# A 31-tap depthwise convolution on VectorE, accumulated in two PSUM banks instead of in SBUF

## The chip, the cores and the metric

The kernel runs on one core of a Trainium2 chip. The metric is the device time of one execution in microseconds (us), as the median of three executions. TensorE (PE in the profile) multiplies matrices, VectorE (DVE), ScalarE (ACT) and GpSimd (POOL) work on elements, SyncE (SP) only issues transfers. SBUF holds 128 partitions; PSUM has eight banks of 128 x 512 fp32.

## What is computed

One layer of a diffusion backbone. The latent stream has 1024 tokens of width 1024, on a grid of 16 rows of 64; there are 256 context tokens. The first half of the layer is

```python
def seq_conv(x, w, b, grid):
    bsz, length, ch = x.shape
    if grid:
        rows = length // GRID_W
        return dwconv(x.reshape(bsz * rows, GRID_W, ch), w, b).reshape(bsz, length, ch)
# mixing: h = modulate(rms_norm(x, g), shift, scale); one projection h @ w gives
#   a, gl         -> u = a * sigmoid(gl) -> seq_conv, width 31 along a grid row -> LayerNorm -> swish
#   q, k, v, gates -> 4 chunkwise mLSTM heads, both directions, started from the context's states
#   o             -> sigmoid gate of the heads' output
# both groups joined -> output projection; then an up/down feed-forward stage
# shift, scale and gates of each stage: six vectors of 1024, a product of silu(c) with w_ada
```

The convolution has 512 channels: four blocks of 128 partitions with 1024 tokens each. An output column of a row is a sum over up to 31 neighbours in that row.

## The kernel before, in words

**Products.** All data are fp32, and a product is made of three: a matrix is split into a high and a low part (`split`, L131 to L135: ScalarE rounds a raw block, and GpSimd or VectorE takes the difference, L134). The weights of a projection come in blocks of 128 x 1024 (`load_blk`) into a ring of three raw tiles, `rawp`.

**Stages, in order of time.** Up to 75 us: the input, its norm, its transposes, the modulation. 75 to 128: the projections a and gl in four blocks j; `glu_evac` (L271 to L274) writes u[j]. 127 to 215: `vpass` (L540 to L567, the projections of v and of the gates with tokens on the partitions), `ctx_prepare` (L335 to L363: the context rows are transposed on TensorE, L353, taken out of PSUM by L358, and split, L362 and L363) and `gates` (L572 to L657), a chain of short steps that goes to and fro between VectorE and TensorE. 215 to 310: the projections k and q (`proj`, L684), woven with `ctx_states` (L711, L713) and head 0 of `heads` (L784 to L823). Then `conv_norm` (L867 to L892) transposes the convolved channels, normalizes them and transposes them back. 325 to 463: heads 1 to 3, the projections of q and o and a part of the output projection; the first instruction that only this stage has is the head norm, L832. From 463 on: the output projection, the up and the down stage; TensorE is busy there nearly without a break.

**The convolution.** `conv(j)` (L276 to L287) begins with the middle tap on ScalarE, into an SBUF tile `accf[:, j]`, and adds the other 30 taps in place on VectorE, each one an instruction over 128 x 784 to 128 x 1008 elements (L286):

```python
act.activation(out=accf[:, j], in_=u[j], func=AF.Identity, scale=conv_w[:, j, 15:16], ...
dve.scalar_tensor_tensor(out=dst, in0=uv[...], scalar=conv_w[:, j, t:t + 1], in1=dst, ...
```

So a tap reads two SBUF tiles (u and the accumulator) beside the column of weights. All four are issued under the lowest priority.

**The later modulation sums.** `ada_stream` (L242 to L252) loads 32 rows of `w_ada` through the raw ring and sums each with one instruction on VectorE (`mod_sum`, L228: a product of 128 x 1024 with a running sum). `proj` takes two of them at each of its twelve calls (`ada_step(2)`), and `ada_step(100)` behind the heads takes what is left.

**What sets the order.** A scheduler fixes the order of the instructions of each engine when the kernel is built; it fills VectorE's gaps with the low-priority taps. The order of SP's transfers is that of the code. At run time an engine takes its instructions in the fixed order, and one that must wait holds up all behind it. A tile is taken from a pool; where all buffers of a pool are in use, the next user waits. PSUM is two pools of four banks each: `mm` for projections, `tp` for transposes, scores and states.

Of the kernel before, what the change touches and what calls it, by code (L numbers as in the profile page):

```python
# [13 lines left out]
P = 128  # L14
# [16 lines left out]
def hybrid_block(ctx: ExitStack, tc: tile.TileContext, x, cx, cc, small, gb, w_ada,  # L31
# [12 lines left out]
    mm = wide.enter_context(tc.tile_pool(name="mm", bufs=4, space=bass.MemoryType.PSUM))  # L44
    tp = wide.enter_context(tc.tile_pool(name="tp", bufs=4, space=bass.MemoryType.PSUM))
    early = ExitStack()
# [35 lines left out]
    def MM():  # L82
        return mm.tile([P, 512], F32, tag="mm", name="mm")

    def TP():
        return tp.tile([P, 512], F32, tag="tp", name="tp")

    def H2(n=512):
# [187 lines left out]
    def conv(j):  # L276
        uv = u[j].rearrange("p (r c) -> p r c", c=W)
        act.activation(out=accf[:, j], in_=u[j], func=AF.Identity, scale=conv_w[:, j, 15:16],
                       bias=conv_b[:, j:j + 1])
        for t in range(CW):  # L280
            o = t - 15
            if o == 0:
                continue
            lo, hi = max(0, -o), min(W, W - o)
            dst = accf[:, j].rearrange("p (r c) -> p r c", c=W)[:, :, lo:hi]
            dve.scalar_tensor_tensor(out=dst, in0=uv[:, :, lo + o:hi + o], scalar=conv_w[:, j, t:t + 1],  # L286
                                     in1=dst, op0=ALU.mult, op1=ALU.add)  # L287

# [42 lines left out]
    def ada_step(n):  # L331
        for _ in range(n):
            next(ada_g, None)
# [142 lines left out]
    for j in range(2):  # L476
        u[j] = T4()
        for hf in range(2):
            glu_evac(j, hf, *ps0[j, hf])
    accf = wide_tile(4, 2)  # L480
    vw = None
    with prio(100000):
# [196 lines left out]
    def proj(i, evac):  # L679
        w = ahead.pop(i)  # L680
        n = order.index(i) + 1
        if n < len(order):
            ahead[order[n]] = load_blk(order[n])
        ada_step(2)  # L684
        for hf in range(2):
            hi, lo = hT[hf]
            ps = MM()
            yield from mm_block(ps, w, hi, lo)
            evac(hf, ps)
        return w  # L690
# [53 lines left out]
    def mlstm_head(h):  # L744
# [38 lines left out]
        for g in range(2):  # L783
# [9 lines left out]
            for t in range(4):  # L793
# [3 lines left out]
                cs = slice(c * P, (c + 1) * P)  # L797
                pv, pc = TP(), TP()
                nv = pv[:, 0:258].rearrange("p (d n) -> p d n", d=2)
# [66 lines left out]

    def conv_norm():  # L867
        for hf in range(2):
            xh = [T4().rearrange("p (t n) -> p t n", n=512) for _ in range(2)]
# [662 lines left out]
```

## Time and profile before

| | |
|---|---|
| median of three executions | 1196.62 us (1196.0 to 1198.24) |
| the profiled execution | 1197.89 us, its span 1195.8 |
| TensorE busy | 1143.2 us, 96% of the span |
| VectorE busy | 932.0 us, 78% |
| ScalarE busy | 523.7 us, 44% |
| GpSimd busy | 121.3 us, 10% |

The span is the profiler's time from the first to the last instruction; 2.1 us of the execution lie around it, and the profiled execution is 1.27 us above the median. Busy shares are means over the whole span: VectorE's 78% is 98 to 100% in some stages and 60% in others.

### The profile page before, as it was taken

What the parts mean: (1) busy time and instruction counts of PE and PEld (TensorE: products, weight loads), DVE (VectorE), ACT (ScalarE), POOL (GpSimd) and SP (SyncE); (2) the same over time, 40 slices, a digit from 0 to 9 for tenths busy, and PEclk for the clock granted to TensorE, in tenths of its full rate; (3) what the DMA queues carried; (4) which work ended last, traced back from release to release, by engine and by line L of the source; (5) the groups of instructions that cost most, each with busy time, mean ns of one, the idle gap of its engine ahead of it and who ended that gap; (6) DMA issues with size and microseconds to landing.
All of it is one profiled execution on the core that took longest, in us unless ns stands there. A gap on an engine that the chain in (4) does not pass through costs nothing.

```text
span 1195.8 us, 14940 instructions
## 1 busy us (share of the span) xinstructions
PE 1143.2 (96%) x5463; PEld 939.5 (79%) x5463; DVE 932.0 (78%) x1702; ACT 523.7 (44%) x952; POOL 121.3 (10%) x106
## 2 busy tenths in 40 slices
PE   6899898999898999999999999999999999999997
PEld 5788787877687777887787888878888878888885
DVE  4899999999779996568966676676668685995585
ACT  6432222242485454357545344343434355454461
POOL 2634120111302210010000000000000000000000
PEclk9899899999999999999999999999999999999999
DMA  8963110442225412442324231323132159633251
GB/s 305 329 207 121 52 37 1 142 147 65 88 89 176 140 56 89 150 167 89 104 73 132 88 122 55 132 89 132 45 132 93 75 192 391 227 112 117 80 220 71
DMA packets 51823, 153.42 MB, mean 128 GB/s; under 512 B 5589, under 2 KB 5925, under 8 KB 49958
## 3 DMA queue, kind: packets, MB, share of 16 engines
q1 hardware_dynamic: 40662, 132.28, 32.0%
q10 hardware_dynamic: 11088, 20.19, 4.5%
q8 instruction: 43, 0.70, 0.2%
q14 instruction: 30, 0.25, 0.1%
HBM read 123.83 MB, written 28.61 MB: 127 GB/s over the span
## 4 chain that ended last, share of the span: by engine, by line
PE 61%; DVE 6%; ACT 1%; issue 1%; POOL 0%; DVEq 0%; POOLq 0%; ACTq 0%
PE mm L1141 8%; PE mm L1143 8%; PE mm L1142 8%; PE c L1369 3%; PE c L1371 3%; PE c L1370 3%; PE tp L1143 3%; PE tp L1142 3%; PE tp L1141 3%; PE a L1369 3%; PE a L1371 3%; PE a L1370 2%; PE mm L951 2%; PE mm L953 2%; PE mm L952 2%; PE tp L508 2%
## 5 line engine op out<-in xcount | busy, mean ns | idle before, releaser
L286 DVE SCALAR_TENSOR_TENSOR s<-t,sml,s 128x864 f32<-128x864 f32 (+14 forms) x120 | 150.5, 1295 | 0.1
L150 PE MATMUL mm<-s,w 128*128 128x512 f32 (+1 forms) x320 | 126.6, 399 | 0.0
L151 PE MATMUL mm<-s,w 128*128 128x512 f32 (+1 forms) x320 | 124.7, 393 | 0.1
L133 ACT ACTIVATE w<-raw 128x1024 fp32r<-128x1024 f32 x94 | 97.0, 1054 | 20.6 <-DMA raw<-in_w_out_dram 5.3
L1141 PE MATMUL mm<-s,w 128*128 128x512 f32 x264 | 104.9, 397 | 0.7 <-ACT h L1214 0.7
L1142 PE MATMUL mm<-s,w 128*128 128x512 f32 x264 | 104.2, 395 | 0.0
L1143 PE MATMUL mm<-s,w 128*128 128x512 f32 x264 | 104.0, 395 | 0.0
L134 DVE TENSOR_TENSOR w<-raw,w 128x1024 fp32r<-128x1024 f32 x77 | 92.3, 1222 | 1.5 <-PE mm L952 0.8
L154 PE MATMUL mm<-s,w 128*128 128x512 f32 (+1 forms) x320 | 93.2, 400 | 0.0
L141 POOL TENSOR_TENSOR r<-yw,mhalf 128x1 f32<-128x1 f32 x16 | 9.7, 608 | 690.7 <-DVE yw L140 690.7
L1141 PE MATMUL mm<-x,w 128*128 128x512 f32 x176 | 70.5, 401 | 0.7 <-ACT h L1205 0.5
L151 PEld LDWEIGHTS mm<-s,w 128*128 128x128 f32 x320 | 60.9, 190 | 11.6 <-POOL s L265 0.7
L1141 PE MATMUL tp<-s,w 128*128 128x512 f32 x176 | 69.5, 395 | 0.0
L150 PEld LDWEIGHTS mm<-s,w 128*128 128x128 f32 x320 | 61.0, 190 | 10.9
L1142 PE MATMUL tp<-s,w 128*128 128x512 f32 x176 | 69.5, 395 | 0.0
L1143 PE MATMUL tp<-s,w 128*128 128x512 f32 x176 | 69.4, 394 | 0.0
L1142 PE MATMUL mm<-x,w 128*128 128x512 f32 x176 | 69.3, 394 | 0.0
L1143 PE MATMUL mm<-x,w 128*128 128x512 f32 x176 | 69.3, 394 | 0.0
L1197 DVE TENSOR_TENSOR h<-mm,h 128x512 f32<-128x512 f32 x22 | 15.2, 692 | 66.3 <-PE mm L1143 66.3
L1271 ACT ACTIVATE s<-x 128x512 fp32r<-128x512 f32 x62 | 38.4, 628 | 64.1 <-PE a L1371 25.0
L1256 DVE TENSOR_TENSOR s<-x,s 128x512 fp32r<-128x512 f32 x62 | 42.8, 695 | 29.0 <-ACT s L1271 29.0
L154 PEld LDWEIGHTS mm<-s,w 128*128 128x128 f32 x320 | 57.0, 189 | 10.2
(311 smaller groups left out, 2916.6 us busy)
## 6 DMA issues: line engine op xcount, KB each, us to landing
raw<-in_w_up_dram SPq DMA_DIRECT2D x44, 512.0 KB, 4.5
zv<-s ACTq DMA_DIRECT2D x77, 256.0 KB, 3.4
raw<-in_w_ada_dram SPq DMA_DIRECT2D x32, 512.0 KB, 4.2
t<-in_w_ada_dram SPq DMA_DIRECT2D x28, 512.0 KB, 5.8
x<-zv SPq DMA_DIRECT2D x14, 1024.0 KB, 5.0
raw<-in_wblk_dram SPq DMA_DIRECT2D x20, 512.0 KB, 4.8
d<-in_w_down_dram SPq DMA_DIRECT2D x28, 256.0 KB, 6.8
x<-zv SPq DMA_DIRECT2D x7, 768.0 KB, 4.2
```

The lines of the kernel that those rows point to most:

```text
L133: act.activation(out=hi, in_=raw, func=AF.Copy)
L134: (eng or pool).tensor_tensor(out=lo, in0=raw, in1=hi.bitcast(F32), op=ALU.subtract)
L150: pe.matmul(o, w[0][:, k], hi[:, k], start=(k == 0), stop=False)
L151: pe.matmul(o, w[0][:, k], lo[:, k], start=False, stop=False)
L154: pe.matmul(o, w[1][:, k], hi[:, k], start=False, stop=(k == KT - 1))
L286: dve.scalar_tensor_tensor(out=dst, in0=uv[:, :, lo + o:hi + o], scalar=conv_w[:, j, t:t + 1], in1=dst, op0=ALU.mult, op1=ALU.add)
L1141: pe.matmul(ps, w[0][:, s], b[0][:, k], start=(start and k == 0), stop=False, skip_group_check=True)
L1142: pe.matmul(ps, w[0][:, s], b[1][:, k], start=False, stop=False, skip_group_check=True)
L1143: pe.matmul(ps, w[1][:, s], b[0][:, k], start=False, stop=(k == 3), skip_group_check=True)
L1369: pe.matmul(ps, o[:, 0, s], o[:, 2], start=start, stop=False, skip_group_check=True)
L1370: pe.matmul(ps, o[:, 0, s], o[:, 3], start=False, stop=False, skip_group_check=True)
L1371: pe.matmul(ps, o[:, 1, s], o[:, 2], start=False, stop=stop, skip_group_check=True)
```

## The change

The pool `tp` shrinks to two banks, and the two freed banks become one tile of a new pool `cv`. `conv(j)` multiplies the middle tap on VectorE into that tile and adds the taps there; the last tap (offset +1) writes into the SBUF tile `accf`, and a copy brings the one column that it does not cover. As `cv` has one buffer, the four convolutions run one after another, where before they ran in pairs. Two memsets claim the SBUF tiles of `accf` ahead of the convolutions. Before the convolutions (`conv_live` empty) the transposes may use halves of a `cv` tile; while they run there are two `tp` banks only, and head 0 takes its second tile from `mm`; from `conv_norm` on the two banks are a pool `tp2` that takes turns with `tp`. `proj` takes no modulation sums in its first five calls and four in each of the other seven.

```diff
-    tp = wide.enter_context(tc.tile_pool(name="tp", bufs=4, space=bass.MemoryType.PSUM))
+    tp = wide.enter_context(tc.tile_pool(name="tp", bufs=2, space=bass.MemoryType.PSUM))
+    cvs = wide.enter_context(ExitStack())
+    cv = cvs.enter_context(tc.tile_pool(name="cv", bufs=1, space=bass.MemoryType.PSUM))
...
+    def CV():
+        return cv.tile([P, 2, 512], F32, tag="cv", name="cv")
+    conv_live = []
+    halves_left = []
+    tp_turn = [0]
     def TP():
+        if conv_live != [True]:
+            tp_turn[0] += 1
+            if conv_live and tp_turn[0] % 2:
+                return conv_live[0].tile([P, 512], F32, tag="tp2", name="tp")
+            if not conv_live and tp_turn[0] % 4 in (3, 0):
+                if not halves_left:
+                    pair = CV()
+                    halves_left.extend((pair[:, 1], pair[:, 0]))
+                return halves_left.pop()
         return tp.tile([P, 512], F32, tag="tp", name="tp")
+    def HP():
+        return MM() if conv_live == [True] else TP()
...
     def conv(j):
         uv = u[j].rearrange("p (r c) -> p r c", c=W)
-        act.activation(out=accf[:, j], in_=u[j], func=AF.Identity, scale=conv_w[:, j, 15:16],
-                       bias=conv_b[:, j:j + 1])
-        for t in range(CW):
+        pair = CV().rearrange("p h n -> p (h n)")
+        pv = pair.rearrange("p (r c) -> p r c", c=W)
+        fv = accf[:, j].rearrange("p (r c) -> p r c", c=W)
+        dve.tensor_scalar(out=pair, in0=u[j], scalar1=conv_w[:, j, 15:16], scalar2=conv_b[:, j:j + 1], op0=ALU.mult,
+                          op1=ALU.add)
+        for t in (*range(15), *range(17, CW), 16):
             o = t - 15
-            if o == 0:
-                continue
             lo, hi = max(0, -o), min(W, W - o)
-            dst = accf[:, j].rearrange("p (r c) -> p r c", c=W)[:, :, lo:hi]
+            dst = (fv if o == 1 else pv)[:, :, lo:hi]
             dve.scalar_tensor_tensor(out=dst, in0=uv[:, :, lo + o:hi + o], scalar=conv_w[:, j, t:t + 1],
-                                     in1=dst, op0=ALU.mult, op1=ALU.add)
+                                     in1=pv[:, :, lo:hi], op0=ALU.mult, op1=ALU.add)
+        dve.tensor_copy(out=fv[:, :, W - 1:W], in_=pv[:, :, W - 1:W])
...
     accf = wide_tile(4, 2)
+    for j in (0, 2):
+        dve.memset(accf[:, j, 0:1], 0.0)
+    conv_live.append(True)
...
-        ada_step(2)
+        ada_step(4 if n > 5 else 0)
...
-                pv, pc = TP(), TP()
+                pv, pc = TP(), HP()
...
     def conv_norm():
+        cvs.close()
+        conv_live[0] = wide.enter_context(tc.tile_pool(name="tp2", bufs=2, space=bass.MemoryType.PSUM,
+                                                       reuse_waits="tile"))
```

In the changed file `glu_evac` ends at L298, the first step of a convolution is L305 and a tap L312; lines behind them stand 27 to 33 further on (L353 is L380, L358 is L385, L711 is L741, L832 is L862).

VectorE at the start of the convolutions, before (t_725 and t_732 are u of blocks 0 and 1, s_739 the SBUF tile that holds both accumulators, t_815 is u of block 2):

```order
L274 TENSOR_TENSOR t_732<-tp,h_736 128x512
L286 SCALAR_TENSOR_TENSOR s_739<-t_725,sml,s_739 128x16x49
L286 SCALAR_TENSOR_TENSOR s_739<-t_725,sml,s_739 128x16x50
L286 SCALAR_TENSOR_TENSOR s_739<-t_732,sml,s_739 128x16x49
L274 TENSOR_TENSOR t_815<-mm,h_866 128x512
L286 SCALAR_TENSOR_TENSOR s_739<-t_725,sml,s_739 128x16x51
L286 SCALAR_TENSOR_TENSOR s_739<-t_732,sml,s_739 128x16x50
L286 SCALAR_TENSOR_TENSOR s_739<-t_725,sml,s_739 128x16x52
```

and now (t_724 is block 0, cv the PSUM tile):

```order
L298 TENSOR_TENSOR t_731<-cv,h_735 128x512
L305 TENSOR_SCALAR cv<-t_724,sml 128x1024
L312 SCALAR_TENSOR_TENSOR cv<-t_724,sml,cv 128x16x49
L298 TENSOR_TENSOR t_820<-mm,h_871 128x512
L312 SCALAR_TENSOR_TENSOR cv<-t_724,sml,cv 128x16x50
L312 SCALAR_TENSOR_TENSOR cv<-t_724,sml,cv 128x16x51
L312 SCALAR_TENSOR_TENSOR cv<-t_724,sml,cv 128x16x52
```

Blocks 0 and 1 took turns before; now all taps of block 0 stand one behind the other, each on the tile that the one before it wrote, and the first step is VectorE's.

TensorE in `ctx_prepare`, before (each tp tile takes four transposes, t4_1265 and t4_1266 are the context rows, mm tiles are v of one block of tokens):

```order
L558 MATMUL mm_1237<-w_967,s8_115 128x272
L353 MATMUL tp_1282<-ident_83,t4_1265 128x128
...
L353 MATMUL tp_1292<-ident_83,t4_1265 128x128
...
L353 MATMUL tp_1302<-ident_83,t4_1265 128x128
...
L353 MATMUL tp_1312<-ident_83,t4_1265 128x128
...
L556 MATMUL mm_1322<-w_955,s8_112 128x272
```

and now:

```order
L588 MATMUL mm_1246<-w_974,s8_118 128x272
L380 MATMUL tp_1291<-ident_86,t4_1274 128x128
...
L380 MATMUL tp_1301<-ident_86,t4_1274 128x128
...
L586 MATMUL mm_1331<-w_962,s8_115 128x272
...
L586 MATMUL mm_1331<-w_968,s8_116 128x272
L380 MATMUL tp_1311<-ident_86,t4_1274 128x128
...
L588 MATMUL mm_1331<-w_968,s8_118 128x272
...
L380 MATMUL tp_1321<-ident_86,t4_1274 128x128
```

Four tiles were filled in one go; now two, and the third and the fourth come 16 and 20 products of v later.

VectorE behind `gates`, before (dec is the last output of `gates`, w<-tp is a state taken from PSUM):

```order
L657 COPY dec<-tp 128x128
L286 SCALAR_TENSOR_TENSOR s_740<-t_815,sml,s_740 128x16x59
L286 SCALAR_TENSOR_TENSOR s_740<-t_971,sml,s_740 128x16x55
L228 SCALAR_TENSOR_TENSOR raw,mod<-raw,G 128x1024 x2
L286 SCALAR_TENSOR_TENSOR s_740<-t_815,sml,s_740 128x16x58
L286 SCALAR_TENSOR_TENSOR s_740<-t_971,sml,s_740 128x16x56
L286 SCALAR_TENSOR_TENSOR s_740<-t_815,sml,s_740 128x16x57
L711 COPY w<-tp 128x129
L228 SCALAR_TENSOR_TENSOR raw,mod<-raw,G 128x1024
L713 SCALAR_TENSOR_TENSOR w<-w,dec,tp 128x129
```

and now:

```order
L687 COPY dec<-tp 128x128
L312 SCALAR_TENSOR_TENSOR cv<-t_820,sml,cv 128x16x62
L312 SCALAR_TENSOR_TENSOR cv<-t_820,sml,cv 128x16x61
L312 SCALAR_TENSOR_TENSOR cv<-t_820,sml,cv 128x16x60
L312 SCALAR_TENSOR_TENSOR cv<-t_820,sml,cv 128x16x59
L312 SCALAR_TENSOR_TENSOR cv<-t_820,sml,cv 128x16x58
L741 COPY w<-tp 128x129
L312 SCALAR_TENSOR_TENSOR cv<-t_820,sml,cv 128x16x57
L743 SCALAR_TENSOR_TENSOR w<-w,dec,tp 128x129
```

The modulation sums are gone from this place. Over the whole order 8 of the 32 stand ahead of the first head norm (L862) where 14 did (L832), and all 32 ahead of the last head norm in both.

## Rows read from the trace of the kernel before

**Rows 1.** The page's first part: busy time, share of the span, instructions.

```profile
PE 1143.2 (96%) x5463; PEld 939.5 (79%) x5463; DVE 932.0 (78%) x1702; ACT 523.7 (44%) x952; POOL 121.3 (10%) x106
```

**Rows 2.** [...]

```profile
core 0: us, PE busy (x) PEld busy (x) DVE busy (x) ACT busy (x) POOL busy (x), PEclk, DMA share, GB/s
125.00:150.00 25.00, 19.71 (x125) 18.59 (x124) 24.40 (x24) 4.56 (x11) 3.99 (x2) 0.86 0.18 59
300.00:325.00 25.00, 22.06 (x123) 17.47 (x123) 17.83 (x68) 10.58 (x15) 7.50 (x9) 1.00 0.29 106
...
97.60:325.30 227.70, 206.14 (x1208) 178.42 (x1207) 218.48 (x362) 66.29 (x149) 48.72 (x32) 0.97 0.25 81
325.30:463.00 137.70, 130.87 (x723) 108.80 (x722) 121.93 (x444) 79.86 (x201) 21.65 (x13) 1.00 0.35 114
140.50:147.40 6.90, 5.81 (x24) 5.49 (x24) 6.30 (x8) 4.21 (x10) 3.99 (x2) 0.51 0.01 4
```

**Rows 3.** What TensorE waited for, 97 to 325 us: the releaser, us in total, times, the longest.

```profile
PE mm L556 <- DVE t L274: 5.1, 2, 3.6
PE tp L508 <- DVE h L821: 4.5, 4, 1.5
PE tp L508 <- DVE gsc L617: 3.4, 1, 3.4
PE tp L508 <- DVE ccol L601: 1.9, 1, 1.9
```

**Rows 4.** Groups of VectorE's instructions by shape, 97 to 325 us: busy time and mean ns of one, then idle time before.

```profile
L286 DVE SCALAR_TENSOR_TENSOR s<-t,sml,s 128x800 f32<-128x800 f32 x8 | 13.0, 1641 | 0.0
L286 DVE SCALAR_TENSOR_TENSOR s<-t,sml,s 128x784 f32<-128x784 f32 x8 | 12.1, 1518 | 0.0
L286 DVE SCALAR_TENSOR_TENSOR s<-t,sml,s 128x928 f32<-128x928 f32 x8 | 11.6, 1445 | 0.0
L286 DVE SCALAR_TENSOR_TENSOR s<-t,sml,s 128x912 f32<-128x912 f32 x8 | 11.4, 1429 | 0.0
L286 DVE SCALAR_TENSOR_TENSOR s<-t,sml,s 128x880 f32<-128x880 f32 x8 | 11.0, 1380 | 0.0
L286 DVE SCALAR_TENSOR_TENSOR s<-t,sml,s 128x848 f32<-128x848 f32 x8 | 10.9, 1358 | 0.0
L286 DVE SCALAR_TENSOR_TENSOR s<-t,sml,s 128x1008 f32<-128x1008 f32 x8 | 10.0, 1260 | 0.0
L286 DVE SCALAR_TENSOR_TENSOR s<-t,sml,s 128x816 f32<-128x816 f32 x8 | 9.6, 1197 | 0.0
L286 DVE SCALAR_TENSOR_TENSOR s<-t,sml,s 128x832 f32<-128x832 f32 x8 | 8.6, 1079 | 0.0
```

**Rows 5.** Single instructions of VectorE and GpSimd in order of time: start, us, what.

```profile
97.62 3.22 DVE L286 SCALAR_TENSOR_TENSOR s<-t,sml,s 128x784 f32<-128x784 f32 x1
97.60 2.40 POOL L134 TENSOR_TENSOR w<-raw,w 128x1024 fp32r<-128x1024 f32 x1 [16.47 <-ACT w L133]
277.78 2.12 DVE L815 SCALAR_TENSOR_TENSOR dn<-dn 128x2 f32<-128x2 f32 x1
276.73 3.16 POOL L134 TENSOR_TENSOR w<-raw,w 128x1024 fp32r<-128x1024 f32 x1 [15.71 <-ACT w L133]
258.70 0.60 DVE L713 SCALAR_TENSOR_TENSOR w<-w,dec,tp 128x129 f32<-128x129 f32 x2
257.77 3.25 POOL L134 TENSOR_TENSOR w<-raw,w 128x1024 fp32r<-128x1024 f32 x1 [21.66 <-PE mm L154]
```

**Rows 6.** Two taps that follow one another on different blocks (213.88 and 215.04), and two on the same block (267.20 and 268.47).

```profile
213.88 1.23 DVE L286 SCALAR_TENSOR_TENSOR s<-t,sml,s 128x992 f32<-128x992 f32 x1
215.04 1.08 DVE L286 SCALAR_TENSOR_TENSOR s<-t,sml,s 128x848 f32<-128x848 f32 x1
267.20 1.24 DVE L286 SCALAR_TENSOR_TENSOR s<-t,sml,s 128x992 f32<-128x992 f32 x1
268.47 1.27 DVE L286 SCALAR_TENSOR_TENSOR s<-t,sml,s 128x1008 f32<-128x1008 f32 x1
```

**Rows 7.** Other groups, 97 to 325 us, as in rows 4: with a source in PSUM (mm, tp) and without, the first step of a convolution on ScalarE, and the modulation sums.

```profile
L274 DVE TENSOR_TENSOR t<-mm,h 128x512 f32<-128x512 f32 x4 | 2.7, 681 | 0.0
L363 DVE TENSOR_TENSOR s<-h,s 128x512 fp32r<-128x512 f32 x4 | 2.7, 682 | 0.0
L358 DVE TENSOR_SCALAR h<-tp,AB 128x256 f32<-128x256 f32 x8 | 3.9, 534 | 0.0
L278 ACT ACTIVATE s<-t,sml 128x1024 f32<-128x1024 f32 x3 | 3.7, 1243 | 30.9 <-DVE t L274 30.9
L228 DVE SCALAR_TENSOR_TENSOR raw<-raw,G 128x1024 f32<-128x1024 f32 x14 | 16.9, 1216 | 0.1
```

**Rows 8.** The context transposes on TensorE, and VectorE's first step on them.

```profile
150.55 1.91 PE L353 MATMUL tp<-ident,t 128*128 128x128 f32 x16
159.49 1.89 DVE L358 TENSOR_SCALAR h<-tp,AB 128x256 f32<-128x256 f32 x4
```

**Rows 9.** What VectorE waited for: first 97 to 325 us, then 325 to 463.

```profile
DVE cst L878 <- PE tp L508: 4.0, 1, 4.0
...
DVE w L713 <- ACT w L771: 5.2, 1, 5.2
```

## The prediction, as it was put before the result was known

> **What bounds the kernel now.** I read the page's first part before all else: TensorE is busy for 96% of the span, VectorE for 78% [rows 1]. Such means hide stages, so I cut the span into stretches next. From the first tap (97.6 us) to the first head norm (325.3) VectorE is busy 218.5 of 227.7 us, and TensorE only 206.1 [rows 2]. TensorE's missing 21.6 us are waits, and in the list of its waits VectorE's lines stand in front: the GLU products (L274), head 0 (L821), the steps of `gates` (L617, L601) [rows 3]. Each of these stands behind taps in VectorE's fixed order. The granted clock is 0.97 over the stretch, and in 140.5 to 147.4 it is 0.51, the lower of its two levels, just where TensorE has waited for L274 [rows 2, 3]. A mean of 0.97 where the low level is half means that 6% of 227.7 us, some 13.7, ran at half speed: 6.8 us lost. So VectorE sets the pace up to the end of the taps, and TensorE has 21.6 + 6.8 = 28.4 us in reserve there.
>
> Near the end of the stretch this turns: in 300 to 325 VectorE is busy 17.8 of 25, one wait of 4.0 us being for the transposes of `conv_norm` [rows 2, 9]. From 325 to 463 both have gaps (TensorE 130.9, VectorE 121.9 busy of 137.7) [rows 2]. Behind 463 nothing is changed; a gain or loss up to there passes one to one into the end. The sum is made against the profiled execution, 1197.89 us, 1.27 above the median of 1196.62.
>
> **The change, part by part.** *Taps no longer collide with GpSimd.* Taps of one width should last alike. The undisturbed widths of 832 and 1008 columns take 1079 and 1260 ns, 1.03 ns a column [rows 4]. On that line 784, 800, 816, 848, 880, 912 and 928 columns should take 1030, 1046, 1063, 1095, 1128, 1161 and 1178 ns; their means are above by 488, 595, 134, 263, 252, 268 and 267 [rows 4]. With eight taps a width that is 8 x 2.27 = 18.1 us. The single rows say why: the tap at 97.62 lasted 3.22 us beside a GpSimd subtraction (L134) that began at 97.60, and a two-column L815 lasted 2.12 beside one [rows 5]. L713, which takes one operand from PSUM, came twice in 0.60 us while GpSimd was at work [rows 5]: an instruction with one wide SBUF operand isn't held up. A tap will be one of this kind. [...] I don't take it all: GpSimd's subtractions remain, and what stands on VectorE in their time may be another instruction with two SBUF operands, as L815 was. Taps hold about two thirds of the stretch (120 of them at some 1.25 us in 227.7), so of some ten hits one or two should land elsewhere, at 2.12 each: about 3 us. I take **−15**, bounds −18 and −9.
>
> *Dependence.* Two taps on different blocks start 1.16 us apart after a tap of 992 columns; on the same block 1.27 [rows 6]. A tap that needs the one just before costs 0.11 us more. In the changed order 61 taps stand directly behind what they need, in the old one 2: 59 x 0.11 = **+6.5**, bounds 0 and +6.5. [...]
>
> *The first step of a convolution* moves from ScalarE (1243 ns [rows 7]) to VectorE, which has no such row. Nearest are L358, the same operation from PSUM over 256 columns, 534 ns, and a tap of 1008 columns, 1260 [rows 4, 7]. 768 more columns at 1.03 give L358 1.32 us; at half that rate 0.93. I take 1.25 x 4 = **+5.0**, bounds +3.7 and +5.3. ScalarE, 29% busy in the stretch [rows 2], gives back nothing on the path. The four copies of 16 columns and two memsets are short: **+0.5**.
>
> *Later modulation sums.* Eight instead of 14 stand ahead of the first head norm: 6 x 1.14 us (a sum of 1216 ns overlaps its neighbours by some 70) = **−6.9** for this stretch. The six come back between the heads. There VectorE has 15.8 us of gaps [rows 2], 5.2 of them one wait at the entry [rows 9], and by the order TensorE enters that stage with about 6 us more of its projections done. I cost the six there at **0**; without that cover, where each is put ahead of what TensorE waits for, they cost up to +6.9. Their loads come four after each weight block through three raw buffers; the DMA engines are 35% busy there [rows 2], so that too stays at 0.
>
> *PSUM as accumulator.* No row shows VectorE writing PSUM. Reading costs nothing: L274 (one operand from PSUM) 681 ns, L363 (both from SBUF) 682 [rows 7]. A column of scalars read beside the operands costs 60 ns: 1260 for a tap of 1008 columns where the sum with a constant takes 1216 − 16 x 1.03 = 1200 [rows 4, 7]. I take it as the upper bound for a write, 124 x 0.06 = +7.4; below, half as much gained, −3.7, if writes behave better than to SBUF. I take **0**, since the near rows show nothing for the other direction. [...]
>
> *Two banks fewer for transposes.* In `ctx_prepare` TensorE filled four tiles in 1.91 us from 150.55 on, and VectorE came to them at 159.49, 7.0 us after their end [rows 8]. With two banks the third tile waits for that, TensorE having 16 products of v (each about as long as a transpose, so some 2 us) for the meantime: it stands some 5 us, which it has in reserve. But VectorE's L358 for tiles three and four then wait for TensorE in their turn. As an estimate half of it: **+2.6**, bounds 0 and +5.
>
> Sum: −15 + 6.5 + 5.0 + 0.5 − 6.9 + 0 + 2.6 = **−7.3**. TensorE can follow: it must make up 7.3 and the 6 us of work that now lie ahead of or between the transposes of `conv_norm`, 13.3 of 28.4. Execution 1190.6, as a median **1189.3**.
>
> **Rivals.** *PSUM taps are dearer (slower).* At 60 ns a tap the gain is gone; from 80 ns on (124 x 0.08 = 9.9 against 7.3) the kernel is slower by a measurable 0.2%. Such a surcharge would come if a write to PSUM and the read by the next tap lengthen the dependent pairs: at 120 ns, +14.9 − 7.3 = +7.6, 1204. For it: 61 dependent pairs and no row on writes. Against: free reads.
>
> *The collisions move (no change).* If hits fall on what is left with two SBUF operands (−9) and the shortage of banks costs its whole 5 us: −9 + 6.5 + 5.0 + 0.5 − 6.9 + 5 = +1.1, 1197.7. Likewise if the six modulation sums are paid in full between the heads: −7.3 + 6.9 = −0.4, 1196.2. For it: L815 was hit too, and 121.9 of 137.7 is dense. Against: those instructions hold a third of the time.
>
> *Nearly all gains at once (much faster).* All hits vanish (3 more), chained taps are covered by other work or cost half (3 more), the first step is at its low bound (1.3 more): −14.6, 1182; a cheaper PSUM access would add 3.7.
>
> **How the numbers follow.** A measurement of this kernel tells about 0.2%, 2.4 us, from no change. The forecast, 1184.5 to 1194.2 as its own range (dependence and PSUM price each moving it by about 4), has 0.53; much faster 0.13; no change 0.16; slower 0.18. Faster 0.66, same 0.16, slower 0.18. The range 1181 to 1200 leaves out about 0.1 above and 0.07 below.
>
> **What would show it.** Taps (L312) with no duration over 1.4 us beside a running GpSimd; starts of chained taps 1.27 us apart at 992 columns (more is the PSUM price); first steps near 1.25. The last tap ends some 7 to 9 us earlier than 308, the first head norm near 318. TensorE's waits for L274's successor and for L601, L617 shrink, and the half-clock stretch at 140 with them; a new wait appears at the third context tile. If the head norm comes early and the stage up to 463 gives it back, the modulation sums or their loads did it. The prediction is wrong if PSUM taps differ from their SBUF widths by over 50 ns, or if TensorE stays late though VectorE is early.

## The result, and the profile after

The changed kernel takes 1212.11 us (1210.92 to 1215.32) where the kernel before takes 1197.43 beside it: 1.0125 times as long, 95% interval 1.0105 to 1.0144. Forecast were 1189.3 us and a gain of 7.3, in a range up to 1200. It is a loss of 14.7: the direction was wrong. The profiled execution is 1215.32 us, its span 1213.3, 17.5 longer than before. It is the longest of the four executions, 3.2 us above their median, so the 17.5 us that its trace splits up are some 3 more than the 14.7 of the medians.

The page's first part, to be held against [rows 1]:

```profile
PE 1154.5 (95%) x5463; PEld 950.0 (78%) x5463; DVE 932.0 (77%) x1712; ACT 523.9 (43%) x950; POOL 113.6 (9%) x106
```

VectorE's busy time is the same to the tenth. TensorE does the same matmuls in 11 us more busy time: part of them ran slower. Where, the stretches tell (columns as in [rows 2]; PEclk is the granted TensorE clock, 1.00 being full speed). First the kernel before, from 90 us to the first head norm:

```profile
90.00:325.30 235.30, 213.74 (x1241) 184.52 (x1240) 226.08 (x376) 68.49 (x151) 48.73 (x32) 0.97 0.25 83
```

Then the changed kernel: 90 us to its first head norm, from there to its last one, and three stretches at the lower clock:

```profile
90.00:327.30 237.30, 218.49 (x1266) 189.80 (x1265) 216.38 (x370) 65.04 (x147) 43.28 (x32) 0.96 0.21 67
327.30:479.60 152.30, 136.37 (x687) 111.61 (x687) 130.37 (x458) 84.25 (x206) 19.11 (x12) 0.91 0.38 125
...
152.90:159.80 6.90, 3.43 (x16) 3.46 (x17) 6.82 (x14) 1.26 (x2) 0.00 (x0) 0.51 0.00 0
269.00:275.80 6.80, 5.99 (x16) 4.93 (x17) 5.86 (x23) 0.73 (x2) 0.00 (x0) 0.50 0.35 112
453.30:463.50 10.20, 8.00 (x21) 5.71 (x22) 8.64 (x44) 4.63 (x14) 1.01 (x1) 0.50 0.32 104
```

Ahead of the heads VectorE is busy 216.4 us and not 226.1: 9.7 us are gone, where its part of the sum (all but the term of the banks) had promised 9.9. Yet the first head norm comes at 327.3 and not at 318, two later than before. The stage of the heads then takes 152.3 us in place of 137.7 [rows 2], with the clock at 0.91 where it was 1.00: 9% of lost speed, with a low level of half, is 18% of 152.3 us, 27, at half clock, and costs at most some 13.5 (less where TensorE stood idle in that time). So the 17.5 us are 2.0 ahead of the heads, 14.6 between them and 0.9 behind.

TensorE's waits in the changed kernel, first 97 to 327 us, then 327 to 480 (columns as in [rows 3]):

```profile
PE tp L380 <- DVE h L385: 7.2, 1, 7.2
PE mm L174 <- DVE h L851: 3.8, 1, 3.8
PE tp L538 <- ACT t L917: 2.8, 3, 1.9
PE mm L586 <- DVE t L298: 2.0, 1, 2.0
PE mm L174 <- ACT h L735: 1.6, 1, 1.6
...
PE tp L538 <- DVE h L851: 5.9, 4, 1.7
PE tp L538 <- DVE h L862: 5.2, 2, 3.5
```

The waits of `gates` (5.3 us in [rows 3]) are gone, the one for the GLU fell from 5.1 to 2.0. In their place stand two that the kernel before does not have: 7.2 us for the third context tile (L380) and 3.8 for a bank of `mm` that head 0 holds (L174 behind L851). Before each of the two waits ends the clock is at its lower level, and stays there behind it: 152.9 to 159.8 and 269.0 to 275.8. TensorE is busy for 3.43 and 5.99 us of these stretches, half of which full speed would have saved: 1.7 and 3.0 us, by estimate.

### The profile page after: what moved, and what is told of

It is laid out like the page before. It is cut to its first block, busy times and chain, and to the rows that moved or that the text cites. A ratio compares the mean times of both kernels' runs of the same rounds, so it can differ in the third digit from the quotient of the medians.

```text
span 1213.3 us, 14916 instructions
## 1 busy us (share of the span) xinstructions
PE 1154.5 (95%) x5463; PEld 950.0 (78%) x5463; DVE 932.0 (77%) x1712; ACT 523.9 (43%) x950; POOL 113.6 (9%) x106
## 4 chain that ended last, share of the span: by engine, by line
PE 75%; DVE 17%; issue 3%; ACT 3%; POOL 1%; DMA 1%; DVEq 0%; SPq 0%; POOLq 0%; ACTq 0%
PE mm L1174 8%; PE mm L1175 8%; PE mm L1176 8%; PE tp L538 4%; PE mm L174 4%; PE mm L175 3%; DVE t L252 3%; PE c L1402 3%; PE c L1403 3%; PE c L1404 3%; PE tp L1174 3%; PE tp L1176 3%; PE tp L1175 3%; DVE cv L312 3%; PE mm L178 3%
## 5 line engine op out<-in xcount | busy, mean ns | idle before, releaser
L174 PE MATMUL mm<-s,w 128*128 128x512 f32 (+1 forms) x320 | 130.4, 411 | 5.4 <-DVE h L851 3.8
L312 DVE SCALAR_TENSOR_TENSOR cv<-t,sml,cv 128x784 f32<-128x784 f32 (+14 forms) x116 | 133.2, 1148 | 2.1
L174 PEld LDWEIGHTS mm<-s,w 128*128 128x128 f32 x320 | 62.8, 196 | 17.5 <-DVE h L851 4.2
L175 PEld LDWEIGHTS mm<-s,w 128*128 128x128 f32 x320 | 62.6, 196 | 13.1 <-POOL s L289 1.9
L178 PEld LDWEIGHTS mm<-s,w 128*128 128x128 f32 x320 | 57.2, 189 | 11.1
```

The lines of the kernel that those rows point to most:

```text
L174: pe.matmul(o, w[0][:, k], hi[:, k], start=(k == 0), stop=False)
L175: pe.matmul(o, w[0][:, k], lo[:, k], start=False, stop=False)
L178: pe.matmul(o, w[1][:, k], hi[:, k], start=False, stop=(k == KT - 1))
```

## The experiments

All ratios are to the kernel before on the same chip. The first head norm (n1), the last one (n2) and the stage between them, in us of the profiled execution, were read from each trace:

| | us | ratio (95%) | n1 | n2 | stage |
|---|---|---|---|---|---|
| before | 1197 to 1198 | 1 | 325.3 | 463.0 | 137.7 |
| the change | 1212.1 | 1.0125 (1.0105 to 1.0144) | 327.3 | 479.6 | 152.3 |
| e1 its sums as before | 1214.5 | 1.0145 (1.0124 to 1.0165) | 333.4 | 478.8 | 145.4 |
| e2 sums late, alone | 1205.7 | 1.0066 (1.0051 to 1.0081) | 321.9 | 461.4 | 139.5 |
| e3 banks, alone | 1212.3 | 1.0124 (1.0109 to 1.0139) | 334.5 | 475.6 | 141.1 |
| e4 first step on ScalarE | 1210.2 | 1.0109 (1.0094 to 1.0124) | 324.1 | 476.3 | 152.2 |
| e5 context tiles from mm | 1208.7 | 1.0093 (1.0067 to 1.0118) | 323.2 | 475.5 | 152.3 |
| e6 before, two pools of two | 1200.2 | 1.0024 (1.0012 to 1.0036) | 325.4 | 466.8 | 141.4 |
| e7 useless products | 1210.7 | 1.0110 (1.0095 to 1.0125) | 325.7 | 472.7 | 147.0 |
| e8 without the last row | 1203.0 | 1.0037 (1.0024 to 1.0050) | 326.8 | 466.4 | 139.6 |
| e12 e3 with e5's edit | 1209.0 | 1.0092 (1.0076 to 1.0108) | 329.4 | 470.7 | 141.3 |
| e13 before, useless products | 1201.8 | 1.0041 (1.0027 to 1.0055) | 323.9 | 461.5 | 137.6 |
| e15 three mends | 1196.9 | 0.9992 (0.9978 to 1.0006) | 319.2 | 464.4 | 145.2 |
| e18 and turns for head 0 | 1194.2 | 0.9973 (0.9961 to 0.9984) | 315.9 | 460.9 | 145.0 |

**Taking the change apart.** Theory A blames the modulation sums put off, B the transpose banks in two pools of two, C an order in which TensorE enters the heads with more projections done. e1 is the change with the sums as before, e2 the kernel before with the sums alone put off, e3 the change's pools with the convolution in SBUF and the sums as before.

```diff
e1 (on the changed kernel)
-        ada_step(4 if n > 5 else 0)
+        ada_step(2)
e2 (on the kernel before)
-        ada_step(2)
+        ada_step(4 if n > 5 else 0)
e3 (on the changed kernel): ada_step(2), and conv() as in the kernel before
```

> The changed kernel with the modulation sums taken as before, two at each projection (14 of 32 ahead of the first head norm, not 8). Theory A, the six sums put off fill the stage of heads 1 to 3 (152.3 us in the changed kernel, 137.7 before) until TensorE waits and its clock falls: that stage comes back to 138 to 142 us, the stretch ahead of it grows by at most 7, and the time lies between 1199 and 1206. Theory B, the stage is longer because four transpose banks are now two pools of two: it stays at 150 or more and the time at 1210 or above. Theory C, it is longer because TensorE's order enters it with more projections done: also unchanged, 1210 or above.

> The kernel before with the modulation sums alone put off (none at the first five projections, four at the others); convolution in SBUF, four transpose banks in one pool. Theory A: the stage of the heads grows from 137.7 us by 8 to 14, with half-clock stretches in it, the stretch ahead gains at most 7: 1200 to 1206. Theories B and C: the stage stays within 2 us of 137.7 and the time falls to 1190 to 1197.

> The changed kernel's pools (two transpose banks while the convolutions run, two pools of two behind) with the convolution in SBUF as before and two modulation sums at each projection: the price of the banks alone. Theory B: 1205 to 1212, most of it in the stage of the heads. Theory A: the wait at the third context tile (7.2 us in the changed kernel) and the half clock behind it show, but VectorE, which sets the pace, loses at most 5: 1196 to 1202, and the stage of the heads stays within 3 us of 137.7.

No theory had it right. The pools alone cost 15 us (e3: 1212.3), all that the change loses. The convolution in PSUM on top of them gives +2.2 (e1 against e3), the sums put off then −2.4 (the change against e1); the intervals overlap in both, so neither is sure. But on the kernel before the same sums cost 8.5 (e2): n1 comes 3.4 us earlier and n2 1.6, and some 10 us are lost behind n2, where the order leaves TensorE 36 matmuls more. Just ahead of n2 it waits once for 6.1 us (e2, 440 to 465 us):

```profile
PE tp L508 <- DVE h L832: 6.1, 1, 6.1
```

In e3 the loss is ahead of the heads: n1 is 9.2 us late. Its waits of TensorE, 97 to 334.5 us:

```profile
PE tp L377 <- DVE h L382: 7.5, 1, 7.5
PE tp L535 <- DVE gsc L644: 4.8, 1, 4.8
PE mm L583 <- DVE t L298: 4.3, 2, 3.6
PE mm L174 <- DVE h L848: 3.8, 1, 3.8
PE tp L535 <- DVE w L738: 3.6, 1, 3.6
PE tp L535 <- DVE dn L842: 3.0, 1, 3.0
```

L377 is the third context tile, L848 head 0's last step on the borrowed bank; L738 and L842 hold transpose banks too. So the shortage shows with the convolution still in SBUF; the waits for L644 (`gates`) and L298 (the GLU) are those of [rows 3], which stay here. In e3 and e1 TensorE's work between n1 and n2 differs (columns as in [rows 2]; e3 first, then e1):

```profile
334.50:475.60 141.10, 133.34 (x728) 110.28 (x727) 123.68 (x443) 79.69 (x203) 21.61 (x12) 1.00 0.34 109
```

```profile
333.40:478.80 145.40, 133.16 (x685) 109.02 (x685) 124.82 (x445) 81.50 (x204) 20.95 (x12) 0.93 0.34 109
```

Same pools, same number of sums, yet e1 has 43 matmuls fewer to do there, falls to 0.93 and takes 4.3 us longer. That fits theory C's reading of the stage, and e7 tests it.

**The two waits ahead of the heads.** e4 puts the first step of a convolution back on ScalarE, which writes the PSUM tile; e5 takes the third and fourth context tile from `mm`; e11 is e5 with head 0's second tile from the two transpose banks; e12 is e3 with e5's edit.

```diff
e4
-        dve.tensor_scalar(out=pair, in0=u[j], scalar1=conv_w[:, j, 15:16], ...
+        act.activation(out=pair, in_=u[j], func=AF.Identity, scale=conv_w[:, j, 15:16], bias=conv_b[:, j:j + 1])
e5, e11, e12 (ctx_prepare)
-            ps = TP()
+            ps = TP() if k2 < 2 else MM()
e11 (mlstm_head)
-                pv, pc = TP(), HP()
+                pv, pc = TP(), TP()
```

> The changed kernel with the first step of each convolution on ScalarE, which writes the PSUM tile. Four steps of 1.35 us leave VectorE; ScalarE's first steps stand ahead of its weight splits again, so GpSimd's subtractions at 91 us should start later and the sums at 91 to 101 us not last 2.3 to 3.4 us. If VectorE sets the pace ahead of the heads, the first head norm comes 5 to 10 us earlier and the time is 1202 to 1207; if TensorE does by now, the time stays within 3 us of 1212.

> The changed kernel with the third and fourth context tile in the pool mm, so that the transposes of the context no longer wait for a free bank. If the 7.2 us wait and the 3.4 us lost at half clock behind it hold up the end, the first head norm comes 6 to 10 us earlier and the time falls to 1202 to 1206; if VectorE sets the pace there, as the prediction had it, the wait is in TensorE's reserve and the time stays within 3 us of 1212.

> The changed kernel with the third and fourth context tile from mm, and head 0's second tile from the two transpose banks and not from mm. In the run without this edit TensorE waits 3.8 us for a bank of mm that head 0 holds, and runs at half clock behind it. If that loan of mm is what costs, the wait goes and the time falls by 3 to 6 us from 1208.7; if two banks for head 0 cost as much in another place, it stays within 3 us of that or rises.

> The changed pools with the convolution in SBUF and two sums at each projection, with the third and fourth context tile from mm. If the wait at the third tile and the half clock behind it are most of the 15 us that the pools cost, the time falls from 1212.3 to 1200 to 1205; if the cost is spread over several waits, to 1206 to 1210.

e4 brings n1 3.2 us earlier and the time 2 lower, less than expected and not clear of noise; e5 4.1 and 3.4, its interval still overlapping the change's. e12 gives the same 3.3 on e3, and there the intervals part. So a wait that the prediction put into TensorE's reserve holds up the end, with some 3.3 of its 7.2 us, fewer than e5's first case had it. e11 came to 1210.5 us (n1 326.3): head 0 on two banks costs 3.1 us more ahead of the heads than the loan of `mm`, the stage gives 2.6 back (149.7 us), and the time can't be told from e5's. Of the pools' 15 us the context takes 3.3; the rest is spread, as e12's second case had it.

**The stage of the heads.** e6 gives the kernel before two pools of two that take turns; e7 adds 27 matmuls that nobody reads behind o1 to o3; e8 leaves out the eight sums of the last row with their loads; e13 is e7's edit on the kernel before; e16 closes both transpose pools at `conv_norm` and opens one of four.

```diff
e6 (on the kernel before)
+        tp_turn[0] += 1
+        if tp_turn[0] % 2:
+            return tp2.tile([P, 512], F32, tag="tp2", name="tp")
e7, e13 (proj)
+        if i in (17, 18, 19):
+            ps = MM()
+            for k in range(9):
+                pe.matmul(ps, w[0][:, k % 8], hT[1][0][:, k % 8], start=True, stop=True)
+                yield
e8
-    ada_g = ada_stream((..., (0, 2, None), (0, 5, None)), RAW)
+    ada_g = ada_stream((..., (0, 2, None)), RAW)
+    dve.memset(mod[:, 0, 5], 0.0)
e16 (conv_norm)
         cvs.close()
+        tps.close()
-        conv_live[0] = wide.enter_context(tc.tile_pool(name="tp2", bufs=2, ...
+        conv_live[0] = wide.enter_context(tc.tile_pool(name="tp2", bufs=4, ...
```

> The kernel before with its four transpose banks as two pools of two that take turns, all else unchanged. If the split into two pools is what costs time between the heads (3.4 us longer there with the changed pools and the convolution in SBUF), the time rises by 3 to 6 us; if four banks are four banks, it stays within 2.4 us of before.

> The changed kernel with 27 products of 128x512 more, whose results nobody reads (6.3 us at full clock), behind the projections o1 to o3, in the stage of the heads. If that stage (152.3 us) is long because TensorE has run out of other work, waits and falls to half clock, the filler costs at most 2 us or shortens it, as the half-clock stretches (27 us long in all) shrink: 1206 to 1214. If TensorE's own work sets the pace, the time rises by 6 to 1218.

> The changed kernel without the eight modulation sums of the last row and without their loads (that row is set to zero, a part of the computation is left out): 16 sums between the heads, fewer than the 18 before. Theory A (the sums fill that stage): the stage falls from 152.3 us to 140 to 144 and the time to 1200 to 1204. If other causes lengthen it, it falls by at most 3 us: 1209 or more.

> The control for the useless products: the same 27 of them behind o1 to o3 in the kernel before, whose stage of the heads has no half-clock stretch and TensorE busy for 130.9 of 137.7 us. If the changed kernel's stage shrank with them because its TensorE had no other work and fell to half clock, the same products must cost here: 3 to 6 us, 1200 to 1204. If they cost nothing here either, the shorter stage there was another effect of the order.

> The changed kernel with both transpose pools closed at the norm of the convolution and one pool of four banks opened in their place. If two pools that take turns lengthen the stage of the heads (3.7 us in the kernel before with two pools throughout), the time falls by 2 to 5 us from 1212; if not, it stays within 2.5 us.

The stage in e7, in e8 and in the control e13 (as in [rows 2]):

```profile
325.70:472.70 147.00, 134.98 (x713) 110.12 (x712) 130.38 (x456) 83.83 (x206) 19.07 (x12) 0.97 0.40 128
```

```profile
326.80:466.40 139.60, 127.51 (x680) 104.35 (x680) 122.66 (x441) 84.06 (x206) 19.52 (x13) 0.97 0.32 106
```

```profile
323.90:461.50 137.60, 130.47 (x722) 108.73 (x721) 120.81 (x439) 78.61 (x200) 22.57 (x13) 1.00 0.34 110
```

In the profiled executions e7 does 26 matmuls more than the change in this stage and needs 5.3 us less for it: the clock is 0.97 and not 0.91. The medians differ by 1.4 us only (1210.7 against 1212.1, their intervals overlap), so what is sure of the whole kernel is that it is no slower: some 6.3 us of useless work were free (an estimate: 27 products at the rate of 73 in 17.0 us, at full clock from 463 to 480 us in the kernel before). On the kernel before, at full clock, the same work costs 3.5 to 5 us (e13): its stage stays at 137.6 us, and what the useless products displaced follows behind the last head norm. So the stage in the changed kernel lacks work that TensorE can do while the heads' steps go to and fro, and with it the clock.

e8 shows what makes the gaps. Without eight sums and their loads VectorE has 7.7 us less to do there, and the stage falls by 12.7: more than the sums themselves, as half-clock stretches go with them (the clock is 0.97 and not 0.91). The loads are a part of this experiment that no run takes alone. VectorE waits for them in the changed kernel (327 to 480 us), in the kernel before not at all:

```profile
DVE raw L252 <- DMA raw<-in_w_ada_dram: 4.9, 3, 2.8
```

In e8 it still waits 4.0 us for the loads that are left, so this wait is not what the 12.7 us come from. On the kernel before, six sums moved behind the last head norm are worth 1.8 to 3.9 us of the stage (e14 and e9, below). Two pools in place of one cost 0.24% of the time, some 2.9 us (e6), and one pool of four opened late (e16, ratio 1.0191) came to 1220.8 us: the stage stays at 150.8 us, and 8 us more are lost behind it, where 16 more matmuls were left over, about half of it. So B is at most a small part of the stage's length. Why the pool opened late costs so much behind the stage stays open.

**Mends.** e9 issues the last row's sums behind the loads of the output projection, in the kernel before; the gate row needs a tile of its own then, which costs the pool h2 two of eight buffers. e14 takes it from the pool t4 in place of that. e10 and e15 are the change with e4, e5 and these two in turn, e17 is e15 with `ada_step(2)`, e18 is e15 with head 0's second tile in turns from `mm` and the transpose banks.

```diff
e9, e10, e14, e15, e17, e18
-    ada_g = ada_stream((..., (0, 2, None), (0, 5, None)), RAW)
+    ada_g = ada_stream((..., (0, 2, None)), RAW)
+    ada_5 = ada_stream(((0, 5, None),), RAW)
...
     mix_split(range(4, 8))
+    run(ada_5)
e14, e15, e17, e18 (gate_row)
-        G = SM(1024, "G", bufs=1)
+        G = t4.tile([P, 1024], F32, tag="G2", ...) if ch == 2 else SM(1024, "G", bufs=1)
e18 (mlstm_head)
-                pv, pc = TP(), HP()
+                pv, pc = TP(), TP() if t % 2 else HP()
```

> The kernel before with the eight modulation sums of the last row issued behind the loads of the output projection, so that 24 to 26 instead of 32 stand ahead of the last head norm (the gate row gets a tile of its own, for which the pool h2 gives two of its eight). If the sums hold up the stage of the heads in the kernel before as in the changed one, it shrinks from 137.7 us by 2 to 6 and the time falls to 1190 to 1195. If VectorE's gaps cover them there, the time stays within 2.4 us of before.

> The kernel before with the last row's eight sums behind the output projection's loads, and the gate row's tile taken from the pool t4 (nine buffers for ten), so that h2 keeps its eight. If the 12 us lost behind the heads in the run that took two buffers from h2 came from these two, the gain at the last head norm (4.7 us there) stays: 1191 to 1195. If the late loads or sums themselves hold up the output projection, 1200 or more.

> The changed kernel with three mends: the third and fourth context tile from mm, the first step of a convolution on ScalarE, and the last row's sums behind the output projection's loads. The parts measured alone were worth 3.4, 2 and (left out altogether) 9 us. If they add up, 1196 to 1200; if they cover one another, 1201 to 1205.

> The changed kernel with the three mends, the gate row's tile from t4 and h2 at its eight. The profile of the run with h2 at six had the last head norm at 465.4 us, 2.4 behind the kernel before, and lost 10 us behind it. If those were h2's, the time is 1198 to 1202, so the convolution in PSUM is still no gain; below 1195 it would be one.

> The changed kernel with the three mends and two sums at each projection (14 ahead of the first head norm, as before the change, 10 between the heads). If the sums cost as much ahead of the heads as between them once the banks are mended, the time stays within 2.4 us of the 1196.9 with four late; if the stage of the heads is the dearer place (one of the eight sums left out there was worth 1.6 us), it falls to 1189 to 1194.

> The changed kernel with the three mends, head 0's second tile in turns from mm and from the transpose banks. The wait of 3.8 us for a bank of mm at 262 us, and the half clock behind it (6.8 us long), are the largest that the run with the three mends has ahead of the heads. If the turns take them away, 1191 to 1195; if head 0 waits for the two transpose banks in their place, within 2.4 us of 1196.9.

e9 took 1206.6 us though its stage is 133.8 us long and n2 4.7 us early. What it gained it lost behind the heads, most of it in the up stage, where TensorE waits on h2, which I had made smaller (560 to 600 us; L1117 makes its weights out of an h2 tile):

```profile
PE tp L1143 <- ACT w L1117: 4.6, 1, 4.6
PE mm L1143 <- ACT h L1216: 1.4, 1, 1.4
PE mm L1143 <- ACT s L1052: 1.0, 1, 1.0
```

e14, with h2 whole, has no such wait and comes to 1199.0, ratio 1.0006 (0.9996 to 1.0015): no gain in the kernel before. Its n2 is 1.5 us early, and 3.0 are lost behind it. e10 fell into the same trap as e9 (1209.2); e15 is level with the kernel before, and its first head norm at 319.2 us is near the forecast 318, though with the first steps on ScalarE. Of the eight sums that the third mend moves only four stand behind n2 there and in e18. e17 (1200.4, 1.0028, interval 1.0018 to 1.0038) says that sums spread evenly are some 4 us worse than late ones once the banks are mended, which neither case expected. e18 beats both kernels: 1194.2 us, 0.9973 (0.9961 to 0.9984). Its stretches up to and between the head norms, and TensorE's waits up to 316 us:

```profile
97.60:315.90 218.30, 205.86 (x1233) 178.14 (x1232) 198.35 (x356) 68.05 (x150) 37.95 (x31) 1.00 0.21 67
315.90:460.90 145.00, 134.29 (x696) 109.30 (x696) 125.61 (x448) 79.99 (x204) 18.72 (x12) 0.95 0.34 115
```

```profile
PE tp L538 <- ACT t L917: 3.3, 4, 1.9
PE tp L538 <- DVE h L851: 2.4, 3, 0.9
PE mm L586 <- DVE h L595: 1.8, 2, 1.6
PE mm L174 <- ACT h L735: 1.3, 1, 1.3
```

No wait of 3.8 or 7.2 us is left, the clock is 1.00 up to n1, and n1 stands 9.4 us ahead of the kernel before. Between the heads it still takes 7.3 us more.

## Why the prediction was wrong, point by point

**VectorE's terms were right, their sum with some luck.** The taps in the changed kernel, by shape as in [rows 4], and the first step:

```profile
L312 DVE SCALAR_TENSOR_TENSOR cv<-t,sml,cv 128x928 f32<-128x928 f32 x8 | 9.5, 1186 | 0.2
L312 DVE SCALAR_TENSOR_TENSOR cv<-t,sml,cv 128x832 f32<-128x832 f32 x8 | 8.7, 1088 | 0.2
L312 DVE SCALAR_TENSOR_TENSOR cv<-t,sml,cv 128x800 f32<-128x800 f32 x8 | 8.4, 1052 | 0.0
L312 DVE SCALAR_TENSOR_TENSOR cv<-t,sml,cv 128x784 f32<-128x784 f32 x8 | 8.3, 1035 | 0.2
L305 DVE TENSOR_SCALAR cv<-t,sml 128x1024 f32<-128x1024 f32 x4 | 5.4, 1348 | 0.1
L312 DVE SCALAR_TENSOR_TENSOR cv<-t,sml,cv 128x1008 f32<-128x1008 f32 x4 | 5.1, 1267 | 0.0
```

No tap is held up any more: 784 columns take 1035 ns and not 1518, and the longest of all 120 lasts 1.27 us. The price of PSUM is 7 to 9 ns a tap (1267 against 1260 for 1008 columns, 1088 against 1079 for 832), about nothing, as forecast. Three taps of 992, 976 and 960 columns that ran into GpSimd's subtraction of 217.25 to 219.65 us took 1.25, 1.24 and 1.22 us. For taps the sentence of the prediction on one wide SBUF operand held. For such instructions in general it did not: L374, with one operand of 128x1024 in SBUF, took 2.76 us at 140.06, just behind the start of a GpSimd subtraction (139.89), and 0.73 at 142.83, after its end; in the kernel before, the same pair (L347) took 2.87 at 144.42, beside a subtraction from 144.36 on, and 0.74 at 147.29. The first step takes 1.35 us, where 1.25 was put. A chained tap:

```profile
106.52 1.05 DVE L312 SCALAR_TENSOR_TENSOR cv<-t,sml,cv 128x800 f32<-128x800 f32 x1
107.61 1.07 DVE L312 SCALAR_TENSOR_TENSOR cv<-t,sml,cv 128x816 f32<-128x816 f32 x1
```

It starts 1.09 us after one of 800 columns; the step of 1.16 at 992 columns without a dependence [rows 6], less 192 columns at 1.03 ns, is 0.96. The dependence costs 0.13, where 0.11 was put. A step that needs the one before it costs something here, so the lower bound of 0, which no run shows, would have been wrong for this term. The convolution's part was −15 + 6.5 + 5.0 + 0.5 = −3.0: from e3 to e1, the same pools and sums, VectorE's busy time from 90 us to n1 falls from 225.5 to 222.7 us, by 2.8 (e3 first, then e1):

```profile
90.00:334.50 244.50, 214.91 (x1227) 187.17 (x1226) 225.49 (x375) 69.08 (x151) 47.35 (x32) 0.93 0.24 78
```

```profile
90.00:333.40 243.40, 219.32 (x1264) 190.04 (x1263) 222.66 (x382) 64.69 (x147) 43.17 (x32) 0.96 0.24 78
```

The sums were put at −6.9; from e1 to the change it falls by 6.3 more. That 9.7 us came for a forecast of 9.9 is in part luck. The dependence was some 1.2 us dearer (59 pairs at 0.13), the first steps 0.4, and the sums brought 0.6 less; what gave these 2 us back on VectorE stays open.

**The collisions did move,** and to a place that was not named. Before, ScalarE's weight split stood behind the first step of a convolution, which waited for VectorE:

```profile
95.33 1.24 ACT L278 ACTIVATE s<-t,sml 128x1024 f32<-128x1024 f32 x1 [6.71 <-DVE t L274]
96.48 1.05 ACT L133 ACTIVATE w<-raw 128x1024 fp32r<-128x1024 f32 x1
```

ScalarE no longer has that step, so GpSimd starts at 91.4 and not at 97.6 [rows 5] and meets the sums of the context's modulation (L252) and a small sum of VectorE (L260; other instructions stand between these):

```profile
91.57 3.31 DVE L252 SCALAR_TENSOR_TENSOR t<-t,t 128x1024 f32<-128x1024 f32 x1
94.81 3.40 DVE L252 SCALAR_TENSOR_TENSOR t<-t,t 128x1024 f32<-128x1024 f32 x1
98.75 2.37 DVE L252 SCALAR_TENSOR_TENSOR t<-t,t 128x1024 f32<-128x1024 f32 x1
101.65 1.30 DVE L260 TENSOR_TENSOR AB<-mod,sml 128x8 f32<-128x8 f32 x1
...
91.40 5.74 POOL L158 TENSOR_TENSOR w<-raw,w 128x1024 fp32r<-128x1024 f32 x2 [9.86 <-ACT w L157]
97.10 5.83 POOL L409 TENSOR_TENSOR w<-raw,w 128x816 fp32r<-128x816 f32 x2
```

Against the usual 1.22 us of such a sum the three lose 5.4 us. e4 undoes the cause in part: GpSimd starts at 92.5 there, but its next subtraction only at 101.8, behind the first step that is ScalarE's again. One such sum is hit, at 93.0 us (3.41 us), and n1 is 3.2 us earlier, with VectorE also rid of the first steps. In the sum the moved hits were put at 3 us, so the term of −15 was still about right; but "ScalarE gives back nothing on the path" was not: it gave GpSimd an earlier start, on the path.

**The first step that failed is that of the two transpose banks.** It was put at +2.6, with "it stands some 5 us, which it has in reserve". The banks measured +15 (e3), and these 12 us are more than half of the 22 between the forecast and the result. In time the convolution's part is +2.2 for −3.0 and that of the sums −2.4 for −6.9 (neither sure, see above). The wait at the third tile was foreseen, 7.2 us in place of 5. The half clock with it was not priced (1.7 us by the estimate above, not the 3.4 that the expectation of e5 names). Nor was head 0, whose second tile blocks `mm` for the projections (3.8 us, and 3.0 more by the half clock); it did not enter the sum at all. And the reserve was none. TensorE's 28.4 us of waits and lost clock would have shrunk had those waits only ended. In the changed kernel, from 97.6 us to the first head norm, 18.8 us of waits (229.7 less 210.9) and a clock of 0.96 are left:

```profile
97.60:327.30 229.70, 210.88 (x1234) 183.65 (x1233) 208.78 (x365) 61.53 (x144) 37.08 (x30) 0.96 0.20 64
```

By the prediction's own working that clock stands for some 9 us lost, so 28 us are still there: the new waits took the old ones' place. It is the last of its signs of being wrong, TensorE late though VectorE is early. With the banks mended and the first steps on ScalarE (e15, e18) VectorE's gain does reach the first head norm: 6.1 and 9.4 us there.

**The second is the stage of the heads, put at 0** with a bound of +6.9. It measured +14.6. The cover was counted in two quantities that did not cover: VectorE's gaps (15.8 us), which I now read as parts of chains of short steps that TensorE waits for (no run shows this alone), and "about 6 us more of its projections done", which was read as an advantage. Those projections were what TensorE did while it waited. With them gone (e1: 43 matmuls fewer than e3) and 24 sums in the stage in place of 18, it waits in many small pieces and falls to half clock in part of the stage (0.93 on average in e1, 0.91 in the change). The loads of the sums, put at 0 too, made VectorE wait for 4.9 us. e8 (−12.7 us of stage without eight sums) and e7 with its control e13 bear out both halves. How the 14.6 us split between sums and missing work is not sharp: by single edits they are 6.9 (the change against e1), 4.3 (e1 against e3) and 3.4 (e3 against before), the last about what two pools of two show alone (3.7 in e6's trace, whose execution is 3.2 us above the median of its ten).

On the rivals: PSUM taps are not dearer, the slower case as it was named did not occur. "No change" had the two right places, the shortage of banks and the sums paid in full, but with VectorE's prices alone, and so too small: what was missing is that TensorE's two longest waits ahead of the heads were paid again in clock, with 1.7 and 3.0 us by the estimate above. The range ended at 1200 for that reason.

## What to carry to other kernels

Whoever takes PSUM banks from one user for another should list, for each tile of the poorer pool, which instruction frees it and what stands ahead of that one on its engine, and price the wait on the engine that waits, its clock included. An engine's idle time is a reserve only if the waits that make it up are removed and none comes in their place. Work that an engine does while it waits is worth keeping for the stretch where it waits; some useless work put there is a quick test of whether a stage is short of work or of speed.

## What the runs showed of the hardware

In the profiled executions TensorE finished a stage in 5.3 us less with some 6.3 us more work in it, as less of its time there was at half clock (granted clock 0.97 for 0.91); by the medians that work was free. And VectorE accumulated in PSUM at the price of SBUF, within 9 ns a tap, and none of the 120 taps with one wide operand in SBUF was held up beside GpSimd, where means of up to 1641 ns stood before [rows 4]. Another instruction with one wide operand in SBUF was: L374 took 2.76 us beside a GpSimd subtraction and 0.73 without one. A tap that reads what the one just before it wrote starts later than one that doesn't, by 0.13 us in the pair shown.
